# A two-layer hybrid trunk: where the GLA heads' projections stand in the order of work

## The chip, the cores and the metric

The kernel runs on one core of one Trainium2 chip. The time is the device time of one execution in microseconds; less is better. TensorE (PE) multiplies matrices, VectorE (DVE) and ScalarE (ACT) do the rest, GpSimd (POOL) a little, and SyncE (SP) issues the loads.

## The reference, cut to what matters

Two layers over 512 tokens (256 context, 256 latent) of width 1024; the second layer needs the latent tokens' outputs alone. Each layer has three token mixers side by side and an MLP:

```python
lx, ly, gq, gk, gv, gr, gz, aq, ak, av, bg = split(h @ w_in)
y1 = rglru_branch(lx, ly, ...)    # convolution, gates, two linear scans (one a direction)
y2 = gla_branch(gq, gk, gv, gr, gz, ...)   # 4 heads, two directions, chunks of 64
y3 = gqa_branch(aq, ak, av, ...)
x = x + ga1 * merge_branches(y1, y2, y3, bg, w_branch, w_out)
x = x + ga2 * squared_relu_mlp(...)
# gla_branch, one head and direction:
g = log_sigmoid(z @ gate_w + gate_b) / 16; b = cumsum(g) in a chunk
scores = tril((q * exp(b - b_mid)) @ (k * exp(b_mid - b)).T)
o = scores @ v + (q * exp(b)) @ s_prev
s = exp(b_last) * s + (k * exp(b_last - b)).T @ v
y2 = rms_norm(o) * silu(r)
```

## The kernel before

Everything is float32. A projection is multiplied as three products of a high and a low part in the float32r type: `weight` (L191) loads one tile of 128 x 1024 into `wraw`, ACT rounds it to `wh` (L200), DVE subtracts to `wl` (L201); three buffers each. `gemm` (L252) makes 24 matmuls of one tile into one of four PSUM banks of the pool `ps_mm`. `gemm_tok` (L276) makes four token blocks at once, 96 matmuls of 512 columns over four weight tiles, and takes all four banks. Layer 1 asks for 256 columns where only latent tokens are needed.

Temporaries come from three pools: `tmp` (`t2`, ten tiles of 128x512), `tmp1` (`t1`, fifteen of 128x256) and `gtmp` (`g2`, three of 128x512, used for the gate tiles of `merge` and in the MLP). An instruction that takes a tile waits until a tile of its pool is free. Each engine, and SP's queue of loads, runs its own list in order. The lists are drawn up when the kernel is built: program order gives the priority (`weight` moves its load and split some 800 instructions ahead), and what is not ready by the builder's own estimate gives way to what is.

The RG-LRU loop (L621) goes over eight channel tiles in pairs: `lru_conv` is a GEMM with a four-tap convolution on ACT and DVE, `lru_gates` four float32 matmuls (eight matmul instructions) with Tanh on ACT, `lru_decay` Exp on ACT, then one Sqrt for the pair (L630), some `gate_y` GEMMs, and `lru_scan` on DVE with a cast on ACT (L293). After pair 2 comes `gla_z`: it loads and splits a small weight (`wz`, `wzs`) and multiplies z (L568). After pair 6 come `gla_gates(0)`: gate matmuls (L598), Abs, Exp and Ln on ACT (L601 to L605), scans on DVE.

Then `gla(h)` runs for four heads: its gates, the K GEMM with an ACT copy (L653), the Q GEMM with an ACT copy (L656), V by `gemm_tok` for each two heads with ACT copies (L661); for each direction the decayed products on DVE and ACT (L677 to L710), the scores (L715, L717), the transposes of the decayed K (L728) into `kt`, and the state products (L741); then the outputs (L760), their norm (L762 to L767, with a power on POOL at L136), and for each half the R GEMM with its SiLU (L771, L772), the transposes (L775), and the product into y2 (L776). After heads 1 and 2 four `merge` calls each multiply y1 by its branch weight (two GEMMs, a Tanh at L787, a product on DVE). Attention follows: keys and values first, then queries, with merges between. Where the trace calls a tile `mm` it is a GEMM's bank, `mx` a bank of the other four, `t` a temporary, `lru` the RG-LRU's work tiles, `yp` the halves of y in layer 1.

In layer 1 the modulation of the layer is still being summed on DVE between this work; its loads (L330) stand in SP's queue among the weights and take `t2` tiles.

Of the kernel before, what the change touches and what calls it, by code (L numbers as in the profile page):

```python
# [15 lines left out]
F32 = mybir.dt.float32  # L16
F32R = mybir.dt.float32r
# [12 lines left out]
QORD = "q0mmfq1mmmfummm", "q0mmfq1mmmmmmf"  # L30
WSPB, EBB, G2B, WRB = 3, 1, 3, 3
NSPL = 5
# [4 lines left out]
NHP = 800  # L37
GZP, G0P = 2, 6
AHEAD = 800
# [65 lines left out]
def trunk_kernel(ctx: ExitStack, tc: tile.TileContext, out: bass.AP, d: dict):  # L105
# [47 lines left out]
    G.memset(cs, 0.0)  # L153
    c8 = const.tile([128, KT, 2], F32, name="c8")
    nc.sync.dma_start(c8, d["cs"])
# [7 lines left out]

    pick = const.tile([128, 2, 32], F32, name="pick")
    G.memset(pick, 0.0)
    for b in range(2):
        G.memset(pick[:, b, b:b + 1], 1.0)

# [4 lines left out]

    th = const.tile([128, KT, 2], F32, name="th")
    S.activation(th, c8, AF.Tanh, scale=0.5)
# [145 lines left out]
    def mods(l, us, pace, nd=KT):  # L321
# [19 lines left out]
        for u, j in halves:  # L341
            bs = (0, 1) if l == 0 or u < 2 else (1,)
            acc = [tmp() for _ in bs]
            terms = [(pick[:, b, :], a) for a, b in zip(acc, bs)]
            nx = load(u, j, 0)
            for k in range(KT):
                t, nx = nx, load(u, j, k + 1) if k + 1 < KT else None
                if k >= nd:
                    terms.append((cs[:, k, :], t))
                    continue  # L350
                for a, b in zip(acc, bs):
                    c = cs[:, k, b:b + 1]
                    if k == 0:
                        S.activation(a, t, AF.Copy, scale=c)
                    else:
                        V.scalar_tensor_tensor(a, t, c, a, op0=ALU.mult, op1=ALU.add)  # L356
# [91 lines left out]
    c2 = const.tile([128, NL, 2, 16], F32, name="c2")  # L448
    lam = const.tile([128, NL, 16], F32, name="lam")
    la = const.tile([128, NL, 16], F32, name="la")  # L450
    lb = const.tile([128, NL, 16], F32, name="lb")
    lc = const.tile([128, NL, 16], F32, name="lc")
    lo_, hi_ = PCOLS["lam"]
    V.tensor_copy(lam, par[:, :, lo_:hi_])
    S.activation(la, lam, AF.Abs)
# [15 lines left out]

    habx = const.tile([128, NL, 32], F32, name="habx")
    lo_, _ = PCOLS["ab"]
    _, hi_ = PCOLS["xb"]
    V.tensor_scalar(habx, par[:, :, lo_:hi_], 0.5, None, op0=ALU.mult)

    for l in range(NL):
# [62 lines left out]
        def lru_scan(i):  # L540
# [15 lines left out]
            split_to(y1h[:, i, c0:], y1l[:, i, c0:], y)  # L556

        def gla_z():


            wz = tmp1(F32, (128, KT, 32))
            nc.sync.dma_start(wz, d["wz"][l])
            wzs = t2.tile([128, KT, 64], F32R, name="wzs", tag="t2")
            split_to(wzs[:, :, :32], wzs[:, :, 32:], wz)
            pz = mx()
# [21 lines left out]
        def gla_gates(h):  # L587
# [26 lines left out]
            return bs  # L614

        LYS = LYS0, LYS1
        ly = iter(range(8))
# [3 lines left out]
        for i in range(0, 8, 2):  # L621
            lru_conv(i + 1)
            lru_gates(i)
            if i < 6:
                lru_conv(i + 2)
            lru_gates(i + 1)
            for j in range(2):
                lru_decay(i + j)
            tt = ws_[1][:, i % 4:i % 4 + 2]
            S.activation(tt, tt, AF.Sqrt, scale=0.25, bias=epsc)  # L630
            for j in range(LYS[l][i // 2 + 1]):
                gate_y(next(ly))
            for j in range(2):
                lru_scan(i + j)
            if i == GZP:
                zs = gla_z()
            if i == G0P:
                gates0 = gla_gates(0)

# [5 lines left out]

        v2 = {}

        def gla(h):
            bs = gla_gates(h) if h else gates0

            pk = gemm(weight(l, "in", O_GK + 128 * h), hh, hl, 0)
            k_ = tmp()
            cp(E_K)(k_, pk)  # L653
            pq = gemm(weight(l, "in", O_GQ + 128 * h), hh, hl, c0)
            q_ = tmp()
            S.activation(q_[:, c0:], pq, AF.Copy, scale=128.0 ** -0.5)  # L656
            if h % 2 == 0:
                for t, ps in gemm_tok(l, O_GV + 256 * h, hh, hl, range(4)).items():
                    for a in range(2):
                        v2[h + a, t] = tmp1()  # L660
                        cp(E_V)(v2[h + a, t], ps[:, 256 * a:256 * a + 256])  # L661
            v_ = [v2.pop((h, t)) for t in range(4)]

            lo = c0 // 64
            nq = 8 - lo
            t0 = c0 // 128
            st = [[None] * 4 for _ in range(2)]
            pts, qhs = [], []
            for dd in range(2):
# [57 lines left out]
                for t in seq[:3]:  # L727
                    P.transpose(pkt[:, 128 * t:128 * t + 128], kh[:, 128 * t:128 * t + 128], ident)  # L728
                kt = tmp()
                if dd == 0:  # L730
                    cp(E_KT)(kt[:, :384], pkt[:, :384])
                else:
                    S.copy(kt[:, :256], pkt[:, :256])
                    S.copy(kt[:, 384:], pkt[:, 384:])
                cur = None
                for j, t in enumerate(seq):
# [28 lines left out]
            for t in range(t0, 4):  # L765
                o = on[t - t0]
                V.tensor_scalar(o, o, rs[:, t:t + 1], None, op0=ALU.mult)  # L767
            for j in range(2):
                pr = gemm(weight(l, "in", O_GR + 256 * h + 128 * j), hh, hl, c0)
                y = tmp()  # L770
                S.activation(y[:, c0:], pr, AF.Tanh, scale=0.5)  # L771
                V.scalar_tensor_tensor(y[:, c0:], y[:, c0:], 1.0, pr, op0=ALU.add, op1=ALU.mult)  # L772
                po = mx()
                for t in range(t0, 4):
                    P.transpose(po[:, 128 * t:128 * t + 128], on[t - t0][:, 128 * j:128 * j + 128], ident)  # L775
                V.scalar_tensor_tensor(y[:, c0:], po[:, c0:], hg[:, j:j + 1], y[:, c0:],  # L776
                                       op0=ALU.mult, op1=ALU.mult)
                split_to(y2h[:, 2 * h + j, c0:], y2l[:, 2 * h + j, c0:], y[:, c0:])

# [15 lines left out]

        m = x[:, :, :256] if last else bigp.tile([128, KT, T], F32, name="big")
        for h in range(4):
            gla(h)
            for i in range(MG[l][h], MG[l][h + 1]):
                merge(0, i, y1h, y1l)  # L800
# [28 lines left out]
        for t, ps in gemm_tok(l, O_AK, hh, hl, range(4)).items():  # L829
# [5 lines left out]
            V.tensor_copy(a, ps[:, 256:])  # L835
            av.append(a)
        rsk = sm.tile([128, 8], F32, name="rsk")
        rsqrt(rsk, ssk, 1.0 / 128, EPS)
# [299 lines left out]
```

## Time and profile before

| what | value |
|---|---|
| median of 3 runs | 1898.92 us (1896.93 to 1903.13) |
| profiled execution | 1897.52 us; its span 1895.7 us |
| busy: PE | 1810.9 us (96%) |
| busy: DVE | 1282.9 us (68%) |
| busy: ACT | 924.8 us (49%) |
| mean granted TensorE clock | 0.989 of full |

The span reaches from the first to the last instruction. Matmuls are pipelined and their ends are modelled, so that PE's share is above its rate of work; a hole is told by the idle time in front of an instruction, which stands in brackets behind its row with what ended it.

### The profile page before, as it was taken

The page shows a single profiled execution, that of the slowest core. Times are in us where ns is not written, and L with a number is a line of the kernel's source. Part 1 is how long each engine was busy: PE and PEld are TensorE (multiplying, and loading weights), DVE is VectorE, ACT ScalarE, POOL GpSimd, SP SyncE. Part 2 cuts the span into 40 slices and gives each one's busy share as a digit, 9 for nine tenths or more (in the row PEclk, how much of TensorE's full clock was granted, in tenths as well). Part 3 has the DMA queues.
Part 4 walks back from the last instruction along what each step waited for, and adds up shares of the span by engine and source line. Part 5 has one row for each costly group of instructions (what it writes and reads, how often), then busy time and mean ns, then how long its engine had stood idle before and what let it go on. Part 6 is the DMA issues. An engine that isn't in the chain of part 4 may idle for free.

```text
span 1895.7 us, 26828 instructions
## 1 busy us (share of the span) xinstructions
PE 1810.9 (96%) x10248; PEld 1509.6 (80%) x10248; DVE 1282.9 (68%) x2177; ACT 924.8 (49%) x1586; POOL 57.1 (3%) x88
## 2 busy tenths in 40 slices
PE   5998999999999999999999999996999999999999
PEld 4765778887777888988888889764888878998887
DVE  5677764535566767789744448787765668577877
ACT  3778544334434333564232325876654554455443
POOL 1000000000000000000000001000000000000000
PEclk9999999999999999999999999998999999999999
DMA  9322223222211566666633335531343333664664
GB/s 318 99 74 73 69 69 90 77 93 78 72 51 56 190 193 196 222 224 199 211 109 97 98 102 185 164 114 61 130 122 111 122 123 91 234 193 150 190 190 154
DMA packets 91617, 255.62 MB, mean 135 GB/s; under 512 B 9184, under 2 KB 20576, under 8 KB 91488
## 3 DMA queue, kind: packets, MB, share of 16 engines
q1 hardware_dynamic: 91488, 253.90, 42.6%
q8 instruction: 81, 1.33, 0.3%
q14 instruction: 48, 0.39, 0.1%
HBM read 252.82 MB, written 1.05 MB: 134 GB/s over the span
## 4 chain that ended last, share of the span: by engine, by line
issue 49%; PE 39%; DVE 5%; ACT 4%; POOL 2%; DMA 0%; SPq 0%; POOLq 0%; ACTq 0%; DVEq 0%
PE mm L212 31%; PE mx L212 2%; PE mx L760 1%; PE mx L741 1%; DVE wl L201 1%; ACT wh L200 1%; PE mx L715 1%; PE mx L526 1%; POOL t L425 1%; PE mx L216 1%; DVE lru L546 0%; PE mx L717 0%; DVE lru L545 0%; ACT lru L630 0%; ACT lru L527 0%
## 5 line engine op out<-in xcount | busy, mean ns | idle before, releaser
L212 PE MATMUL mm<-h,wh 128*128 128x512 f32 (+1 forms) x2640 | 733.3, 360 | 8.3 <-DVE wh L198 4.5
L200 ACT CAST wh<-wraw 128x1024 fp32r<-128x1024 f32 x363 | 379.8, 1049 | 544.3 <-PE mm L212 465.3
L201 DVE TENSOR_TENSOR wl<-wraw,wh 128x1024 fp32r<-128x1024 f32 x365 | 445.8, 1223 | 257.6 <-ACT wh L200 254.2
L212 PEld LDWEIGHTS mm<-h,wh 128*128 128x128 f32 x2640 | 468.3, 189 | 85.4 <-issue 6.6
L212 PE MATMUL mm<-h,wl 128*128 128x512 f32 (+1 forms) x1448 | 493.2, 341 | 0.0
L212 PEld LDWEIGHTS mm<-h,wl 128*128 128x128 f32 x1448 | 273.8, 189 | 31.9 <-issue 1.4
L212 PE MATMUL mm<-yh,wh 128*128 128x512 f32 (+1 forms) x640 | 224.7, 351 | 2.4 <-DVE big L957 2.4
L212 PE MATMUL mm<-yh,wl 128*128 128x512 f32 (+1 forms) x640 | 224.3, 350 | 0.0
L212 PE MATMUL mm<-yl,wh 128*128 128x512 f32 (+1 forms) x640 | 222.6, 348 | 0.0
L212 PE MATMUL mm<-wh,h 128*128 128x512 f32 x576 | 187.3, 400 | 18.5 <-ACT t L653 18.1
L212 PE MATMUL mm<-yp,wh 128*128 128x256 f32 (+1 forms) x704 | 186.0, 338 | 3.8 <-ACT g L787 2.3
L212 PE MATMUL mm<-yp,wl 128*128 128x256 f32 x512 | 144.4, 282 | 0.0
L356 DVE SCALAR_TENSOR_TENSOR t<-t,cs,t 128x512 f32<-128x512 f32 x178 | 127.2, 746 | 24.1 <-DMA t<-mod_w 15.1
L212 PEld LDWEIGHTS mm<-wh,h 128*128 128x128 f32 x576 | 109.7, 191 | 42.3 <-ACT t L653 18.9
L212 PEld LDWEIGHTS mm<-yp,wh 128*128 128x128 f32 x704 | 120.8, 191 | 20.1 <-ACT g L787 2.5
L212 PEld LDWEIGHTS mm<-yh,wh 128*128 128x128 f32 x640 | 121.6, 190 | 17.8 <-issue 3.4
L212 PEld LDWEIGHTS mm<-yh,wl 128*128 128x128 f32 x640 | 121.2, 189 | 15.3 <-issue 0.7
L212 PEld LDWEIGHTS mm<-yl,wh 128*128 128x128 f32 x640 | 121.2, 189 | 15.0 <-issue 0.5
L212 PE MATMUL mm<-wl,h 128*128 128x512 f32 x288 | 115.2, 400 | 2.0 <-DVE wl L201 2.0
L212 PEld LDWEIGHTS mm<-yp,wl 128*128 128x128 f32 x512 | 97.1, 190 | 1.0 <-issue 1.0
L212 PE MATMUL mx<-t,t 128*128 128x128 f32 (+2 forms) x416 | 81.8, 338 | 0.0
L957 DVE SCALAR_TENSOR_TENSOR big<-mm,modT,big 128x256 f32<-128x256 f32 x64 | 28.6, 480 | 66.8 <-PE mm L212 66.8
(226 smaller groups left out, 1987.4 us busy)
## 6 DMA issues: line engine op xcount, KB each, us to landing
wraw<-wt SPq DMA_DIRECT2D x365, 512.0 KB, 3.6
t<-mod_w SPq DMA_DIRECT2D x144, 256.0 KB, 3.8
modw<-mod_w SPq DMA_DIRECT2D x6, 2048.0 KB, 14.1
big<-xt SPq DMA_DIRECT2D x8, 512.0 KB, 5.3
gw<-lruw SPq DMA_DIRECT2D x16, 256.0 KB, 3.5
out<-big SPq DMA_DIRECT2D x8, 128.0 KB, 2.5
t<-glaw SPq DMA_DIRECT2D x8, 96.0 KB, 3.1
t<-ropeg SPq DMA_DIRECT2D x2, 256.0 KB, 3.0
```

The source lines that it names most:

```text
L200: S.copy(wh, r)
L201: (G if lo == "G" else V).tensor_tensor(wl, r, wh.bitcast(F32), op=ALU.subtract)
L212: P.matmul(o, a, b, **kw)
L216: P.transpose(o, a, ident)
L356: V.scalar_tensor_tensor(a, t, c, a, op0=ALU.mult, op1=ALU.add)
L425: G.tensor_tensor(h[:, :n], x[:, k, c0:c1], st[1][:, :n], op=ALU.mult)
L526: P.matmul(pg, gw[:, 2 * dd + q, :], xc, start=True, stop=True)
L715: P.matmul(psc[:, c], en[:, c], em[:, c], start=True, stop=True)
L741: P.matmul(pu[:, :256], kt[:, 128 * t:128 * t + 128], v_[t], start=True, stop=True)
L760: P.matmul(po[:, :256], a, b, start=j == 0, stop=j == len(mm) - 1)
L957: V.scalar_tensor_tensor(x[:, i, c], ps[:, 256 * s - a:256 * s - a + 256], s0[:, i, s:s + 1], x[:, i, c], op0=ALU.mult, op1=ALU.add)
```

## The change

In both layers: the small weight of z is loaded and split at the layer's start, into a tile of the pool `g2`. In the last pair of the RG-LRU loop the order becomes: channel 7's convolution, K and Q of head 0, gates of channel 6, head 0's gates, V of heads 0 and 1, gates of channel 7, decays, Sqrt, the two R GEMMs of head 0 with their SiLU, the scans. `gla(h)` makes R ahead of the scores; its state products come behind both directions' scores; and its end (transposes of the output, the product into y2) is returned as a function, which the next head calls behind its K and Q, or, after head 3, attention behind its key and value copies. `kt` and R's product come from `g2`, which gets a fourth tile. To make room, some constants of the start are temporaries, `pick` is smaller and `habx` is computed in place.

```diff
-WSPB, EBB, G2B, WRB = 3, 1, 3, 3
+WSPB, EBB, G2B, WRB = 3, 1, 4, 3
...
+        wz = tmp1(F32, (128, KT, 32))
+        nc.sync.dma_start(wz, d["wz"][l])
+        wzs = g2.tile([128, KT, 64], F32R, name="wzs", tag="g2")
+        split_to(wzs[:, :, :32], wzs[:, :, 32:], wz)
+
         def gla_z():
...
-            wz = tmp1(F32, (128, KT, 32))
-            nc.sync.dma_start(wz, d["wz"][l])
-            wzs = t2.tile([128, KT, 64], F32R, name="wzs", tag="t2")
-            split_to(wzs[:, :, :32], wzs[:, :, 32:], wz)
...
+        def gla_kq(h):
+            pk = gemm(weight(l, "in", O_GK + 128 * h), hh, hl, 0)
+            k_ = tmp()
+            cp(E_K)(k_, pk)
+            pq = gemm(weight(l, "in", O_GQ + 128 * h), hh, hl, c0)
+            q_ = tmp()
+            S.activation(q_[:, c0:], pq, AF.Copy, scale=128.0 ** -0.5)
+            return k_, q_
...
+        def gla_r(h):
+            ys = []
+            for j in range(2):
+                pr = gemm(weight(l, "in", O_GR + 256 * h + 128 * j), hh, hl, c0)
+                y = gtmp()
+                S.activation(y[:, c0:], pr, AF.Tanh, scale=0.5)
+                V.scalar_tensor_tensor(y[:, c0:], y[:, c0:], 1.0, pr, op0=ALU.add, op1=ALU.mult)
+                ys.append(y)
+            return ys
...
             lru_conv(i + 1)
-            lru_gates(i)
             if i < 6:
+                lru_gates(i)
                 lru_conv(i + 2)
+            else:
+                kq0 = gla_kq(0)
+                lru_gates(i)
+                gates0 = gla_gates(0)
+                v0 = gla_v(0)
             lru_gates(i + 1)
...
+            if i == 6:
+                ys0 = gla_r(0)
             for j in range(2):
                 lru_scan(i + j)
             if i == GZP:
                 zs = gla_z()
-            if i == G0P:
-                gates0 = gla_gates(0)
...
+            if h:
+                bs = gla_gates(h)
+                k_, q_ = gla_kq(h)
+                before()
+                v_ = gla_v(h)
+                ys = gla_r(h)
+            else:
+                bs, (k_, q_), v_, ys = gates0, kq0, v0, ys0
...
-                kt = tmp()
+                kt = gtmp()
...
+                kts.append((kt, decp))
+            for dd, (kt, decp) in enumerate(kts):
+                seq = (0, 1, 2, 3) if dd == 0 else (1, 0, 3, 2)
                 cur = None
...
-            for j in range(2):
-                pr = gemm(weight(l, "in", O_GR + 256 * h + 128 * j), hh, hl, c0)
...
+            def end():
+                for j, y in enumerate(ys):
+                    po = mx()
...
+        end = None
         for h in range(4):
-            gla(h)
+            end = gla(h, end)
...
             av.append(a)
+        end()
```

## Rows read from the trace of the kernel before

**Rows 1.** Windows of both layers: span, busy PE, PEld, DVE, ACT, POOL, clock, DMA
```profile
140.00:475.00 335.00, 317.92 (x1462) 256.97 (x1461) 195.29 (x300) 169.63 (x288) 11.15 (x21) 0.99 0.25 78
1262.00:1530.00 268.00, 241.69 (x1375) 203.07 (x1374) 182.32 (x322) 158.72 (x279) 9.43 (x21) 0.96 0.36 112
```
**Rows 2.** Chain that ended last: start, duration, what; both layers, GEMMs without holes
```profile
369.04 43.57 PE mm L212 x192
...
1459.21 17.99 PE mm L212 x150
```
**Rows 3.** Order of time, PE, layer 0: start, duration, instruction, count, [idle before, releaser]
```profile
157.04 1.03 PE L212 MATMUL mm<-h,wh 128*128 128x512 f32 x2
...
169.21 3.67 PE L526 MATMUL mx<-t,gw 128*128 128x512 f32 x8 [1.61 <-issue]
...
190.09 0.79 PE L212 MATMUL mm<-wh,h 128*128 128x512 f32 x1 [7.65 <-ACT t L653]
```
**Rows 4.** Window of GEMM matmuls (L212) alone: span, PE busy (count), PEld busy, clock
```profile
174.12:182.45 8.33, 8.32 (x37) 6.57 (x35) 1.00 0.27 90
```
**Rows 5.** Order of time, ACT, layer 0, end of the RG-LRU
```profile
177.20 1.28 ACT L630 ACT_TABLE_LOAD   x1
178.50 2.01 ACT L630 ACTIVATE lru<-lru,epsc 128x2048 f32<-128x2048 f32 x1
...
185.33 1.06 ACT L605 ACTIVATE eb<-eb 128x1024 f32<-128x1024 f32 x1
188.93 0.62 ACT L293 CAST yh<-lru 128x512 fp32r<-128x512 f32 x1 [2.54 <-DVE lru L555]
189.46 0.58 ACT L653 COPY t<-mm 128x512 f32<-128x512 f32 x1
```
**Rows 6.** Order of time, PE, layer 1, end of the RG-LRU
```profile
1296.96 6.33 PE L526 MATMUL mx<-t,gw 128*128 128x512 f32 x8 [4.11 <-DVE t L515]
...
1318.27 0.79 PE L212 MATMUL mm<-wh,h 128*128 128x512 f32 x1 [10.41 <-ACT t L653]
```
**Rows 7.** Windows behind the long holes; columns as rows 1
```profile
190.09:193.11 3.02, 3.02 (x7) 2.40 (x8) 3.02 (x6) 0.44 (x1) 0.00 (x0) 0.53 0.03 5
...
1318.27:1322.97 4.70, 4.70 (x12) 3.69 (x12) 4.70 (x8) 0.24 (x1) 0.00 (x0) 0.52 0.02 3
```
**Rows 8.** Waits, layer 0 then 1: us in total, times, longest; ends of heads
```profile
PE mx L775 <- DVE t L767: 3.8, 4, 1.0
...
PE mx L775 <- DVE t L767: 2.3, 4, 0.7
```
**Rows 9.** Waits, layer 0; then order of time, PE, layer 1: scores and merges
```profile
PE mx L715 <- DVE t L709: 2.5, 2, 1.3
...
1367.81 0.50 PE L212 MATMUL mm<-yp,wh 128*128 128x256 f32 x2 [1.50 <-ACT t L653]
1376.13 0.50 PE L212 MATMUL mm<-yp,wh 128*128 128x256 f32 x2 [2.30 <-ACT g L787]
1378.82 1.20 PE L715 MATMUL mx<-t,t 128*128 128x128 f32 x4 [1.18 <-DVE t L709]
```
**Rows 10.** Order of time, PE, both layers: first matmul of z
```profile
128.23 0.66 PE L568 MATMUL mx<-h,wzs 128*64 128x512 f32 x1 [2.62 <-DVE wzs L294]
...
1257.09 0.42 PE L568 MATMUL mx<-h,wzs 128*64 128x512 f32 x1 [1.37 <-DVE wzs L294]
```
**Rows 11.** Order of time, DVE: operands of head 0's first scores, and a wait
```profile
204.42 0.68 DVE L709 TENSOR_TENSOR t<-t,t 128x512 f32<-128x512 f32 x1
...
1309.47 1.29 DVE L545 SCALAR_TENSOR_TENSOR lru<-lru 128x512 f32<-128x512 f32 x2 [4.73 <-ACT lru L630]
...
1334.74 0.41 DVE L710 TENSOR_TENSOR t<-t,t 128x256 f32<-128x256 f32 x1
```
**Rows 12.** Window of GEMM matmuls (L212), head 0, layer 0, scores to output; as rows 4
```profile
206.96:226.28 19.32, 10.19 (x38) 6.90 (x38) 1.00 0.30 88
```
**Rows 13.** Waits of SP's queue in layer 1: us in total, times, longest
```profile
SPq L330 <- DVE lru L555: 18.6, 1, 18.6
```

More of the change, by code (lines that the diff above doesn't have):

```diff
@@ L37 @@
 NHP = 800
-GZP, G0P = 2, 6
+GZP = 2
 AHEAD = 800
@@ L153, in trunk_kernel @@
     G.memset(cs, 0.0)
-    c8 = const.tile([128, KT, 2], F32, name="c8")
+    c8, th = (tmp1(shape=(128, KT, 2)) for _ in range(2))
     nc.sync.dma_start(c8, d["cs"])
@@ L161, in trunk_kernel @@
     G.memset(epsc, 1e-30)
-    pick = const.tile([128, 2, 32], F32, name="pick")
+    pick = const.tile([128, 33], F32, name="pick")
     G.memset(pick, 0.0)
-    for b in range(2):
-        G.memset(pick[:, b, b:b + 1], 1.0)
+    G.memset(pick[:, 1:2], 1.0)
     def pc(l, name, a=0, n=None):
@@ L171, in pc @@
         return par[:, l, lo + a:hi if n is None else lo + a + n]
-    th = const.tile([128, KT, 2], F32, name="th")
     S.activation(th, c8, AF.Tanh, scale=0.5)
@@ L343, in mods @@
             acc = [tmp() for _ in bs]
-            terms = [(pick[:, b, :], a) for a, b in zip(acc, bs)]
+            terms = [(pick[:, 1 - b:33 - b], a) for a, b in zip(acc, bs)]
             nx = load(u, j, 0)
@@ L448, in trunk_kernel @@
     c2 = const.tile([128, NL, 2, 16], F32, name="c2")
[L449 to L452, printed above, removed]
+    la, lb, lc = (tmp1(shape=(128, NL, 16)) for _ in range(3))
     lo_, hi_ = PCOLS["lam"]
-    V.tensor_copy(lam, par[:, :, lo_:hi_])
+    lam = par[:, :, lo_:hi_]
     S.activation(la, lam, AF.Abs)
@@ L469, in trunk_kernel @@
     V.tensor_scalar(c2[:, :, 1, :], lam, 2.0, None, op0=ALU.mult)
-    habx = const.tile([128, NL, 32], F32, name="habx")
     lo_, _ = PCOLS["ab"]
     _, hi_ = PCOLS["xb"]
-    V.tensor_scalar(habx, par[:, :, lo_:hi_], 0.5, None, op0=ALU.mult)
+    habx = par[:, :, lo_:hi_]
+    V.tensor_scalar(habx, habx, 0.5, None, op0=ALU.mult)
     for l in range(NL):
@@ L614, in gla_gates, with gla_v @@
             return bs
+        v2 = {}
+        def gla_kq(h):
[6 more added lines that the diff above has]
+            return k_, q_
+        def gla_v(h):
+            if h % 2 == 0:
+                for t, ps in gemm_tok(l, O_GV + 256 * h, hh, hl, range(4)).items():
+                    for a in range(2):
+                        v2[h + a, t] = tmp1()
+                        cp(E_V)(v2[h + a, t], ps[:, 256 * a:256 * a + 256])
+            return [v2.pop((h, t)) for t in range(4)]
+        def gla_r(h):
[7 more added lines that the diff above has]
+            return ys
         LYS = LYS0, LYS1
@@ L644, in trunk_kernel, with gla @@
         y2h, y2l = ytiles("yl")
[L646 to L662, printed above, removed]
+        def gla(h, before=None):
+            if h:
[6 more added lines that the diff above has]
+                bs, (k_, q_), v_, ys = gates0, kq0, v0, ys0
             lo = c0 // 64
@@ L667, in gla @@
             st = [[None] * 4 for _ in range(2)]
-            pts, qhs = [], []
+            pts, qhs, kts = [], [], []
             for dd in range(2):
@@ L767, in gla @@
                 V.tensor_scalar(o, o, rs[:, t:t + 1], None, op0=ALU.mult)
-            for j in range(2):
-                pr = gemm(weight(l, "in", O_GR + 256 * h + 128 * j), hh, hl, c0)
[L770 to L778, printed above, removed]
+            def end():
+                for j, y in enumerate(ys):
+                    po = mx()
+                    for t in range(t0, 4):
+                        P.transpose(po[:, 128 * t:128 * t + 128], on[t - t0][:, 128 * j:128 * j + 128], ident)
+                    V.scalar_tensor_tensor(y[:, c0:], po[:, c0:], hg[:, j:j + 1], y[:, c0:],
+                                           op0=ALU.mult, op1=ALU.mult)
+                    split_to(y2h[:, 2 * h + j, c0:], y2l[:, 2 * h + j, c0:], y[:, c0:])
+            return end
         m = None
```

## The prediction, made before the changed kernel ran

> **What bounds the kernel now.** I read first the engines' busy time in the two stretches that the change touches, one a layer, from the last RG-LRU gates to the end of the GLA heads [rows 1]. PE is busy for 317.9 of 335 us and 241.7 of 268; DVE for 195.3 and 182.3, ACT for 169.6 and 158.7. TensorE sets the pace, and what an order of work can win is its holes, 17.1 and 26.3 us, and what it lost at half clock behind them. How fast it goes without holes stands in the chain of waits [rows 2]: 192 matmuls in 43.57 us are 0.227 us each (512 columns), 150 in 17.99 are 0.120 (256 columns). A GEMM of one weight tile has 24: 5.4 us over 512 tokens, 2.9 over the 256 of layer 1.
>
> Then PE's order of time, for holes. In layer 0 [rows 3]: 1.61 us ahead of channel 7's gates and 7.65 in the middle of head 0's V, waiting for ACT's copy of K (L653). PE had made K and Q from 157.04, ahead of gates (169.21) that stand before them in the program: the order is put together from what is ready, not taken from the text. V has 96 matmuls over four PSUM banks; 36 were done (the window's 37 hold one of Q) [rows 4] when it needed the banks of K and Q. ACT's order of time tells why they were still held [rows 5]: the square root until 180.5, head 0's Exp and Ln until 186.4, then 2.54 idle behind a cast that waits for the scan on DVE, and only then, at 189.46, the copy of K that could have run 25 us before. Layer 1 has the same holes, larger [rows 6]: 4.11 and 10.41, and the eight gate matmuls after the first took 6.33 us where layer 0 took 3.67. The windows show the granted clock there at about half of full [rows 7], that is 1.2 for 2.4 GHz. The other holes are regular: ahead of the transposes at each head's end, 3.8 and 2.3 us over four heads each [rows 8]; ahead of some heads' scores and layer 1's merges [rows 9]; ahead of the rank-16 gates' z, behind the split of wzs [rows 10].
>
> **The change part by part**, in us of the profiled execution.
>
> (a) wzs is loaded and split at the layer's start instead of in front of z. Both waits go: 2.62 + 1.37 = 4.0. Its load and two small operations move ahead of the first GEMMs, past SP's first weights; that costs between 0 (beside them) and 2.6 (the same wait elsewhere). I take 0.3, since the split is now wanted tens of us later. Gain 3.7.
>
> (b) Layer 0, K and Q with their copies ahead of gates 6, head 0's gates and V ahead of gates 7, R ahead of the scans. The stop goes: 1.61 + 7.65, and the restart at half clock: 7 matmuls took 3.02 [rows 7] against 1.59, so 1.43. Together 10.7. What is late next are head 0's scores. From 182.4 the other 60 V matmuls take 13.6, to 196.0; the two R GEMMs, now next, 48 x 0.227 = 10.9, to 206.9. DVE ended the first direction's operands at 205.1 [rows 11]. So the scores hardly wait, but DVE gets R's two products ahead of the scans, queued behind PE: I keep 10.
>
> (c) Layer 1, the same edits: 4.11 + 10.41, gates at half clock 6.33 - 3.67 = 2.66, restart 4.70 of which some 4.4 at half clock [rows 7], so 2.2. Together 19.4. Here the scores do wait. V stood at 36 of 96 at 1307.9; without 4.11 and 2.66 that is 1301.1, V's end 1314.7, R's (48 x 0.120) 1320.5. DVE had the operands at 1335.2 [rows 11], 14.7 later. The next head's K and Q can fill 5.4 + 2.9 = 8.3, leaving 6.4; DVE's own idle 4.73 behind the square root can go, which leaves 1.7; a stop of that kind costs up to 2.2 more at half clock. Between 0 and 8.6; I take 4. Gain 15.4.
>
> (d) A head's end goes behind the next head's keys, the last one's behind attention's keys and values. The 3.8 + 2.3 = 6.1 are now covered by a GEMM of 5.4 or more. Its products are wanted only by the second branch's merges. It holds two SBUF tiles a head longer (see g). If the order leaves too little between, the 6.1 come back. I take 5.6.
>
> (e) R ahead of the scores gives each head 10.9 or 5.8 us more work before its scores: the 2.5 of layer 0 and two times 1.18 of layer 1 go [rows 9], 4.9. Layer 1's merges waited 1.50 for a late K copy and 2.30 for a gate tile; no edit is aimed at them, 0 to 3.8, and I take 0.6. Gain 5.5.
>
> (f) The price of (b) and (e): R was what PE did between a head's scores and its output, where it else waits for DVE and ACT. In head 0 of layer 0 there were 38 such matmuls in that stretch [rows 12], 8.6 us; at 0.120 in layer 1 4.6. If nothing takes their place: 4 x 8.6 + 4 x 4.6 = 52.8; if all is replaced: 0. The next head's K and Q (10.9, 8.3) stand right behind, merges behind heads 1 and 2, attention's K and V behind head 3, and [rows 3] show that GEMMs are drawn ahead. So nearer to 0: I take 10.
>
> (g) Kt and R's products move to the pool of the merges' gate tiles, four instead of three. While a head is in its state products it holds two Kt and two R: a merge can be multiplied into PSUM, but not be evacuated. Two merges fill the four banks, 21.8 and 11.5 us of work, against a stretch of 19.3 [rows 12]: no wait in layer 0, up to 7.8 at heads 1 and 2 of layer 1. 0 to 15.6; I take 3, since Kt is free before the output.
>
> The constants that become temporaries, the state products behind both directions' scores and the smaller pick tile move no GEMM: 0, beside PE's work.
>
> ACT changes function sets more: head 0's Exp and Ln now stand between the gates' Tanh of channels 6 and 7. One load takes 1.28 us and the next operation follows 0.02 later [rows 5]. At most two more a layer, 5.1 us of an engine that is 51% and 59% busy [rows 1]: 0 on the path. The Trainium skill, ScalarE: Activation LUTs, section Table sets: the hidden batching unit, tells one to group functions by set, which this change goes against, and puts a switch at about 2.66 us with its drain. By that price ACT would have 10.6 us more; the row shows no drain.
>
> **Sum.** 3.7 + 10 + 15.4 + 5.6 + 5.5 - 10 - 3 = 27.2. The profiled execution took 1897.5, and the median is 1.4 above that; 1898.9 - 27.2 = 1871.7, and I forecast 1871.
>
> **The rivals.**
>
> Nothing takes R's place (slower): between scores and output PE idles for DVE and ACT in every head, all 52.8 of (f). The time is 1871 + 42.8 = 1914. It is slower than before from 37 us of the 52.8 on, some 70%. For it: PSUM has four banks for GEMMs, and R's last two are freed only by DVE, which is full there. Against it: [rows 3], and that ACT alone frees K and Q. Chance 0.09.
>
> The stalls move: scores of layer 1 late by the whole 8.6 (4.6 more than charged) and merges held by (g) (12.6 more): 1888. For it: R's products, which wait for PE, now stand ahead of the scans on DVE, and everything of head 0 that DVE does comes after. Chance 0.17.
>
> It doesn't do what it says: K and Q are still copied late, because the pool of ten 512-column tiles is full. For it: a modulation load, which needs such a tile, held SP's queue for 18.6 us in layer 1 [rows 13]. Then 7.65 + 1.43 + 10.41 + 2.2 = 21.7 stay, less the 4.7 already charged on them: 1888. Against it: Kt, R and wzs leave that pool. Chance 0.11.
>
> ACT's loads fall on the path: 5.1 more, 1876. By the page's price named above it would be 10.6 more. Chance 0.05.
>
> All is covered: (f), (g) and the charges in (c) and (e) are nothing, 20 less: 1851. Chance 0.13.
>
> **How the numbers follow.** The forecast has the other 0.45, and its own range is 1860 to 1880. A measurement tells 0.3% from no change, 5.7 us, so faster is below 1893.2. The forecast, full cover and ACT's loads lie there (0.63); of the moved stalls 0.14, of the late copies 0.07: 0.84. Same: 0.03 + 0.04, and 0.01 of the slower one: 0.08. Slower: 0.08. The range 1850 to 1894 leaves out the slower rival (0.09), half of the full cover's spread and a little of the late copies: about 0.16.
>
> **What would show it.** Right: the copy of K follows its GEMM within a few us; no hole over 2 us between channel 7's convolution and head 0's scores in either layer; the granted clock stays at full from gates 7 on; the transposes at a head's end no longer wait for the scaling by the norm; z has no wait. Wrong: PE waiting for head 0's operands by more than 4 us, PE waiting between scores and output (f), merges' matmuls waiting for their gate tiles (g), or the K copy still behind the scan's cast. The prediction fails if PE's order is drawn up so that it has nothing else ready in the heads.

## The result, and the profile after

The changed kernel took 1873.01 us (median of 4 runs, 1869.75 to 1874.93), the kernel before 1900.49 in the runs beside it (4, 1896.93 to 1903.13): a ratio of 0.9855, 95% interval 0.9832 to 0.9878. It is 27.5 us faster; the forecast was 1871. The profiled execution took 1873.47 us with a span of 1871.7.

First the page's engines after the change, then the windows that answer to [rows 1], shifted so that they hold nearly the same work (1448 matmuls for 1462 and 1376 for 1375; span, busy PE, PEld, DVE, ACT, POOL, clock, DMA):

```profile
PE 1806.8 (97%) x10248; PEld 1513.2 (81%) x10248; DVE 1277.6 (68%) x2176; ACT 926.3 (49%) x1586; POOL 65.6 (4%) x87
```

```profile
140.00:455.00 315.00, 309.64 (x1448) 254.32 (x1446) 189.78 (x295) 162.99 (x279) 17.77 (x21) 1.00 0.27 84
1241.40:1500.00 258.60, 236.93 (x1376) 204.51 (x1374) 179.07 (x314) 154.92 (x269) 10.81 (x21) 0.95 0.36 112
```

Layer 0's window has 5.4 us of holes where [rows 1] had 17.1. Layer 1's still has 21.7, where it had 26.3, and its clock fell from 0.96 to 0.95: layer 0 was put right, layer 1 hardly.

How far the layers differ is read from two landmarks on PE that are the same work in every kernel: the first gate matmul of channel 0, and the first transpose of attention's keys. The stretch between them, one a layer:

| kernel | layer 0 | layer 1 |
|---|---|---|
| before | 65.1 to 476.2: 411.1 | 1200.4 to 1529.0: 328.6 |
| after | 64.1 to 455.4: 391.3 | 1179.5 to 1501.4: 321.9 |
| gain | 19.8 | 6.7 |

Behind the second landmark there are 366.7 us before and 370.3 after. No edit reaches there, and in the fourteen kernels shown here that part lies between 366.1 and 371.0. The same program for layer 0 gave its stretch 391.3 here, 391.5, 392.8 and 394.1 in others (pair_mix, v_late1 and scan_late1 below). Each stretch comes from one profiled execution, so a difference under some 3 us tells nothing by itself.

PE's order of time in layer 0 after the change, its only holes above 0.5 us from 150 us to the end of the heads; and ACT's copy of K (start, duration, instruction, count, [idle before, releaser]):

```profile
165.75 1.08 PE L595 MATMUL mx<-zs,t 96*128 96x512 f32 x2 [2.77 <-ACT lru L522]
...
223.67 1.16 PE L743 MATMUL mx<-t,t 128*128 128x128 f32 x8 [0.72 <-DVE t L737]
...
254.72 1.16 PE L743 MATMUL mx<-t,t 128*128 128x128 f32 x8 [0.83 <-DVE t L738]
```

```profile
157.52 0.58 ACT L619 COPY t<-mm 128x512 f32<-128x512 f32 x1
```

The copy of K is made at 157.52, not at 189.46 [rows 5], and the hole of 7.65 in V [rows 3] is gone. In its place stands 2.77 ahead of head 0's gates, released by ACT's Tanh of channel 6 (L522). There is no wait above 0.5 us at the heads' ends, at z, or between a head's second scores and its output; the 0.72 and 0.83 stand ahead of scores.

Layer 1 (L743 are the scores, made for a head's first and then its second direction; L521 here channel 7's gates, L210 a merge):

```profile
1290.55 3.59 PE L521 MATMUL mx<-t,gw 128*128 128x512 f32 x8
...
1299.73 0.61 PE L743 MATMUL mx<-t,t 128*128 128x128 f32 x4
...
1324.97 1.22 PE L743 MATMUL mx<-t,t 128*128 128x128 f32 x4 [9.62 <-DVE t L737]
...
1343.53 0.80 PE L210 MATMUL mm<-yp,wh 128*128 128x256 f32 x2 [3.29 <-ACT t L619]
...
1356.01 1.23 PE L743 MATMUL mx<-t,t 128*128 128x128 f32 x4 [4.05 <-DVE t L738]
...
1362.29 1.19 PE L743 MATMUL mx<-t,t 128*128 128x128 f32 x4 [3.60 <-DVE t L737]
```

The holes of 4.11 and 10.41 [rows 6] have gone. Head 0's first scores run at 1299.73 without a wait, but 9.62 stands ahead of its second, and head 1's scores wait 4.05 and 3.60, where 1.18 stood [rows 9]. Windows of that stretch (columns as above), and DVE's order of time in it:

```profile
1285.00:1303.00 18.00, 18.00 (x106) 14.27 (x105) 9.20 (x17) 15.48 (x26) 0.42 (x2) 1.00 0.39 117
1303.00:1325.00 22.00, 12.38 (x91) 11.37 (x90) 21.61 (x39) 9.97 (x16) 0.92 (x2) 0.85 0.39 121
...
1345.00:1365.00 20.00, 12.35 (x66) 11.09 (x66) 15.38 (x33) 7.76 (x14) 1.38 (x4) 0.67 0.27 83
```

```profile
1287.24 0.43 DVE L737 TENSOR_TENSOR t<-t,t 128x256 f32<-128x256 f32 x1
...
1302.75 1.29 DVE L540 SCALAR_TENSOR_TENSOR lru<-lru 128x512 f32<-128x512 f32 x2 [3.51 <-ACT lru L665]
...
1324.49 0.42 DVE L737 TENSOR_TENSOR t<-t,t 128x256 f32<-128x256 f32 x1
```

In the first window PE has no hole and DVE idles for 8.8 of 18 us; in the second DVE is full and PE idles for 9.6 of 22. So the work came to DVE late. DVE's rows show from where: it had the operands of head 0's first scores at 1287.7 (L737); then the scans of channels 6 and 7 (L540) wait for the square root (L665), and the last operand of the second scores (L737 again, 1324.49) comes behind them.

### The profile page after: what moved, and what is told of

The parts are those of the page before. It is cut to its first block, busy times and chain, and to the rows that moved or that the text cites. A ratio compares the mean times of both kernels' runs of the same rounds, so it can differ in the third digit from the quotient of the medians.

```text
span 1871.7 us, 26774 instructions
## 1 busy us (share of the span) xinstructions
PE 1806.8 (97%) x10248; PEld 1513.2 (81%) x10248; DVE 1277.6 (68%) x2176; ACT 926.3 (49%) x1586; POOL 65.6 (4%) x87
## 5 line engine op out<-in xcount | busy, mean ns | idle before, releaser
L210 PE MATMUL mm<-h,wh 128*128 128x512 f32 (+1 forms) x2640 | 730.4, 360 | 6.4 <-DVE wh L196 3.4
L210 PEld LDWEIGHTS mm<-h,wh 128*128 128x128 f32 x2640 | 468.3, 189 | 85.5 <-issue 6.4
L210 PE MATMUL mm<-h,wl 128*128 128x512 f32 (+1 forms) x1448 | 493.9, 341 | 0.1
L210 PEld LDWEIGHTS mm<-h,wl 128*128 128x128 f32 x1448 | 274.2, 189 | 32.3 <-DVE wl L199 1.2
L210 PE MATMUL mm<-yh,wh 128*128 128x512 f32 (+1 forms) x640 | 224.8, 351 | 2.9 <-ACT wh L198 2.9
L210 PE MATMUL mm<-yh,wl 128*128 128x512 f32 (+1 forms) x640 | 224.1, 350 | 0.0
L210 PE MATMUL mm<-yl,wh 128*128 128x512 f32 (+1 forms) x640 | 222.6, 348 | 0.0
L210 PE MATMUL mm<-yp,wh 128*128 128x256 f32 (+1 forms) x704 | 189.2, 342 | 3.3 <-ACT t L619 3.3
L210 PE MATMUL mm<-wh,h 128*128 128x512 f32 x576 | 183.5, 395 | 0.0
L210 PE MATMUL mm<-yp,wl 128*128 128x256 f32 x512 | 145.9, 285 | 0.0
L210 PEld LDWEIGHTS mm<-yp,wh 128*128 128x128 f32 x704 | 122.1, 193 | 20.3 <-ACT t L619 3.5
L210 PEld LDWEIGHTS mm<-yh,wh 128*128 128x128 f32 x640 | 121.6, 190 | 18.3 <-ACT wh L198 3.1
L210 PEld LDWEIGHTS mm<-yh,wl 128*128 128x128 f32 x640 | 121.2, 189 | 15.5 <-issue 0.7
L210 PEld LDWEIGHTS mm<-yl,wh 128*128 128x128 f32 x640 | 121.2, 189 | 14.9 <-issue 0.5
L210 PEld LDWEIGHTS mm<-wh,h 128*128 128x128 f32 x576 | 107.8, 188 | 22.3 <-issue 0.7
L210 PE MATMUL mm<-wl,h 128*128 128x512 f32 x288 | 113.1, 393 | 0.0
L210 PEld LDWEIGHTS mm<-yp,wl 128*128 128x128 f32 x512 | 98.2, 192 | 1.0 <-issue 1.0
L210 PE MATMUL mx<-t,t 128*128 128x128 f32 (+2 forms) x416 | 81.7, 338 | 0.1
```

The lines of the kernel that those rows point to most:

```text
L210: P.matmul(o, a, b, **kw)
```

## The experiments

Every run below is set beside the kernel before on the same chip. Each part of the change was undone alone (wz_back, end_back, r_back, pair_back), the pair's order was put into the kernel before without the moves of R, ends and load (pair_alone) and into layer 0 alone (pair_mix), and the wait of 9.62 was attacked in four ways (scan_late1, t2_11, kq_first, v_late1 and v_late2); gates_ahead goes at what was left in head 1. The stretches are those of the table above. By the intervals end_back, r_back and pair_alone are slower than the changed kernel. Those of v_late1 and v_late2 touch its own at the edge, and each of their runs (at most 1868.58) was faster than each of its runs (1869.75 and up). The other intervals overlap with its own, so that what is said of these kernels rests on the stretches and on the waits in the rows.

| kernel | median, us | ratio to before, 95% | layer 0 | layer 1 |
|---|---|---|---|---|
| after | 1873.01 | 0.9855 (0.9832 to 0.9878) | 391.3 | 321.9 |
| wz_back | 1871.85 | 0.9858 (0.9838 to 0.9878) | 391.5 | 322.0 |
| end_back | 1882.42 | 0.9911 (0.9889 to 0.9934) | 397.3 | 324.2 |
| r_back | 1888.49 | 0.9940 (0.9918 to 0.9962) | 400.4 | 326.1 |
| pair_back | 1877.16 | 0.9885 (0.9862 to 0.9908) | 401.9 | 317.8 |
| pair_alone | 1892.43 | 0.9948 (0.9929 to 0.9967) | 405.3 | 326.7 |
| pair_mix | 1868.07 | 0.9831 (0.9816 to 0.9846) | 391.5 | 317.8 |
| scan_late1 | 1870.66 | 0.9842 (0.9814 to 0.9871) | 394.1 | 320.0 |
| t2_11 | 1873.57 | 0.9856 (0.9831 to 0.9880) | 392.3 | 320.8 |
| kq_first | 1873.08 | 0.9850 (0.9828 to 0.9872) | 392.5 | 320.4 |
| v_late1 | 1867.12 | 0.9821 (0.9806 to 0.9836) | 392.8 | 313.5 |
| v_late2 | 1865.29 | 0.9814 (0.9795 to 0.9833) | 394.0 | 312.2 |
| gates_ahead | 1867.37 | 0.9832 (0.9815 to 0.9848) | 394.1 | 312.0 |

### wz_back: the small weight loaded in front of z again

```diff
-        wz = tmp1(F32, (128, KT, 32))
-        nc.sync.dma_start(wz, d["wz"][l])
-        wzs = g2.tile([128, KT, 64], F32R, name="wzs", tag="g2")
-        split_to(wzs[:, :, :32], wzs[:, :, 32:], wz)
         def gla_z():
+            wz = tmp1(F32, (128, KT, 32))
+            nc.sync.dma_start(wz, d["wz"][l])
+            wzs = g2.tile([128, KT, 64], F32R, name="wzs", tag="g2")
+            split_to(wzs[:, :, :32], wzs[:, :, 32:], wz)
```

> The changed kernel with the load and the split of z's small weight back in front of z (its tile stays in the larger pool). Forecast's term (a): 3.7 us slower than the changed kernel, so about 1877, with waits of some 2.6 us (layer 0) and 1.4 us (layer 1) ahead of z's first matmul. Rival: the wait was hidden anyway by what else DVE does there and returns as a wait elsewhere: within 1 us of 1873.

Neither stretch moved, and z has no wait in either layer. pair_alone too has its z without a wait with the load in front of it and the tile in `g2`. So the wait of 4.0 [rows 10] is gone, but not through the move; what both runs keep is, among other things, the tile's other pool, with its fourth tile, and `kt` out of `t2`. No run put either back into `t2`, so that this is the cause is not shown.

### end_back: a head's end directly behind its norm

```diff
-                before()
...
-            return end
+            end()
...
-            end = gla(h, end)
+            gla(h)
...
-        end()
```

> The changed kernel with each head's end straight behind its outputs, as before. Forecast's term (d): 5.6 us slower than the changed kernel, about 1879, with eight waits of 0.3 to 1 us for the scaling by the norm. Rival: with R already done, nothing stands between the outputs and the end's transposes, so that each wait is longer than before, 2 us and more a head: about 1890.

9.4 us slower than the changed kernel by the medians, 6.0 + 2.3 by the stretches. PE's waits, layer 0's heads and then layer 1's (us in total, times, longest; L803 are the ends' transposes, L742 the scores):

```profile
PE mx L803 <- DVE t L797: 2.8, 3, 1.0
PE mx L742 <- DVE t L736: 2.6, 3, 1.0
PE mx L803 <- ACT g L817: 1.0, 1, 1.0
```

```profile
PE mx L803 <- DVE t L797: 2.7, 4, 0.8
```

The ends' waits are back with 3.8 in layer 0 and 2.7 in layer 1; [rows 8] had 3.8 and 2.3. The scores of layer 0 wait 2.6 instead of 1.6. That is 7.5 of the 8.3.

### r_back: R behind the scores again

```diff
-            if i == 6:
-                ys0 = gla_r(0)
...
-                ys = gla_r(h)
...
-                bs, (k_, q_), v_, ys = gates0, kq0, v0, ys0
+                bs, (k_, q_), v_ = gates0, kq0, v0
...
+            ys = gla_r(h)
```

> The changed kernel with the two R GEMMs of every head behind its outputs again, head 0's too. By the forecast's (e) and (f) R's place costs 10 - 5.5, so this kernel is up to 4.5 us faster than the changed one, about 1869, with waits ahead of the scores back in layer 0. Rival from the trace of after: in layer 0 R ahead of the scores costs nothing (no hole between scores and output), and R's 10.9 and 5.8 us are wanted ahead of the scores: slower by 5 to 15 us, 1878 to 1888.

15.5 us slower than the changed kernel, 9.1 + 4.2 by the stretches. PE's order of time at head 0's second scores, layer 0 and layer 1:

```profile
221.53 2.08 PE L740 MATMUL mx<-t,t 128*128 128x128 f32 x8 [6.47 <-DVE t L734]
```

```profile
1332.84 1.20 PE L740 MATMUL mx<-t,t 128*128 128x128 f32 x4 [12.13 <-DVE t L734]
```

Without R ahead of a head's scores head 0's second ones wait 6.47 instead of 0.72, and 12.13 instead of 9.62. R is worth more ahead of the scores than behind them.

### pair_back: the old order of the last gates, all else kept

```diff
             lru_conv(i + 1)
+            lru_gates(i)
             if i < 6:
-                lru_gates(i)
                 lru_conv(i + 2)
-            else:
-                kq0 = gla_kq(0)
-                lru_gates(i)
-                gates0 = gla_gates(0)
-                v0 = gla_v(0)
             lru_gates(i + 1)
...
-            if i == 6:
-                ys0 = gla_r(0)
...
+            if i == 6:
+                gates0 = gla_gates(0)
...
+            bs = gla_gates(h) if h else gates0
+            k_, q_ = gla_kq(h)
             if h:
-                bs = gla_gates(h)
-                k_, q_ = gla_kq(h)
                 before()
-                v_ = gla_v(h)
-                ys = gla_r(h)
-            else:
-                bs, (k_, q_), v_, ys = gates0, kq0, v0, ys0
+            v_ = gla_v(h)
+            ys = gla_r(h)
```

> The changed kernel with the last RG-LRU pair in the order of before: head 0's gates behind the scans, its K, Q, V and R behind the loop; ends, R ahead of the scores and z's weight stay as changed. Forecast's (b) and (c): 25 us slower than the changed kernel, about 1898, nearly all of the gain lost, with PE waiting for the copy of K in both layers. Rival: the gain is spread, and this part holds less than half of it: below 1887.

Only 4.1 us slower, and the two layers go opposite ways: layer 0 loses 10.6, layer 1 gains 4.1. PE's order of time:

```profile
161.86 6.66 PE L521 MATMUL mx<-t,gw 128*128 128x512 f32 x8 [3.98 <-issue]
...
185.39 0.79 PE L210 MATMUL mm<-wh,h 128*128 128x512 f32 x1 [3.46 <-ACT t L619]
...
1301.98 0.79 PE L210 MATMUL mm<-wh,h 128*128 128x512 f32 x1 [10.30 <-ACT t L619]
...
1350.16 0.50 PE L210 MATMUL mm<-yp,wh 128*128 128x256 f32 x2 [1.50 <-ACT t L619]
...
1363.19 0.68 PE L735 MATMUL mx<-t,t 128*128 128x128 f32 x4 [1.25 <-DVE t L730]
...
1368.59 1.22 PE L735 MATMUL mx<-t,t 128*128 128x128 f32 x4 [3.87 <-DVE t L729]
```

The stops for the copy of K are back in both layers, 10.30 in layer 1 as in [rows 6]. And yet layer 1 is faster with that stop than with the new order: head 0's scores (here L735) don't wait at all, and the last three rows, head 1's late K copy and its two scores, are 1.50, 1.25 and 3.87, 6.6 in all, where the changed kernel has 3.29, 4.05 and 3.60, 10.9. So the new order exchanged a stop of 10.30 for a wait of 9.62 and made head 1 wait 4.3 longer.

### pair_alone: the pair's new order, but R, ends and load of z's weight where they were before

```diff
-WSPB, EBB, G2B, WRB = 3, 1, 3, 3
+WSPB, EBB, G2B, WRB = 3, 1, 4, 3
...
-            lru_gates(i)
             if i < 6:
+                lru_gates(i)
                 lru_conv(i + 2)
+            else:
+                kq0 = gla_kq(0)
+                lru_gates(i)
+                gates0 = gla_gates(0)
+                v0 = gla_v(0)
```

The diff is against the kernel before. The constants that make room, the pool of z's weight and of `kt`, and the state products behind both directions' scores are as in the changed kernel.

> The kernel before with the new order of the last RG-LRU pair alone (head 0's K, Q, gates and V among the gates): R behind the outputs, ends straight behind, z's weight in front of z. (State products stay behind both directions' scores, and the larger pool stays.) If the parts add up as the four runs before say (layer 0: 10 gained by the pair's order, layer 1: 4 lost), it is 6 us faster than before, about 1894. By the forecast's (b) and (c) it would be 25 us faster, 1875. Rival: without R ahead nothing covers head 0's scores in either layer and it is not faster than before at all: 1899 or more.

About 9 us faster than before: 5.8 in layer 0, 1.9 in layer 1, of which 2.6 and 1.4 may be z's waits. The holes ahead of head 0's second scores are those of r_back, 6.47 and 12.13. So the new order without R ahead of the scores is worth some 3 us in layer 0, with R 10.6.

### pair_mix: the new order in layer 0, the old one in layer 1

```diff
             if i < 6:
                 lru_gates(i)
                 lru_conv(i + 2)
+            elif last:
+                lru_gates(i)
             else:
...
-            if i == 6:
+            if i == 6 and not last:
                 ys0 = gla_r(0)
...
+            if i == 6 and last:
+                gates0 = gla_gates(0)
...
+                v_ = gla_v(h)
+                ys = gla_r(h)
+            elif last:
+                bs = gates0
+                k_, q_ = gla_kq(h)
```

> After's kernel with the new order of the last gates in layer 0 and the order of the kernel before in layer 1. With the old order in both layers TensorE reached the first key transpose of attention 10.2 us later in layer 0 but took 3.9 us less from there to that of layer 1. If the two layers add, this run is about 4 us faster than the changed kernel, 1869; the wait ahead of head 0's scores in layer 1 is then near 10 us as with the old order in both layers. If the gain in layer 1 came only from starting later, the time is the changed kernel's, 1873.

4.9 us faster than the changed kernel by the medians, and the stretches are just layer 0 of the one and layer 1 of the other, 391.5 and 317.8. The layers add. The stop for K stands in layer 1:

```profile
1290.73 0.80 PE L210 MATMUL mm<-wh,h 128*128 128x512 f32 x1 [10.30 <-ACT t L619]
```

### scan_late1: layer 1's last scans behind head 0's operands

```diff
+LATE = (False, True)
...
-                lru_scan(i + j)
+                if not (LATE[l] and i == 6):
+                    lru_scan(i + j)
...
+            if LATE[l] and h == 0:
+                for j in range(2):
+                    lru_scan(6 + j)
...
```

> The changed kernel, but in layer 1 the scans of channels 6 and 7 stand behind both directions' score operands of head 0 instead of ahead of them. Theory DVE: the hole of 9.6 us ahead of the second direction's scores is DVE working through 13 us of scans first; then the hole goes, and the time falls by 8 to 12 us to about 1862. Theory tiles: PE waits there because all four GEMM banks hold results (K, Q and R of head 1) that find no free temporary, so moving the scans only moves the hole: within 3 us of 1873.

In the changed kernel the scans do stand ahead of the second operands, but moving them behind is not enough. PE's order of time:

```profile
1322.62 0.71 PE L747 MATMUL mx<-t,t 128*128 128x128 f32 x4 [0.91 <-DVE t L742]
...
1330.23 1.22 PE L780 MATMUL mx<-t,g 128*128 128x256 f32 x2 [3.85 <-DVE t L785]
...
1333.72 4.41 PE L799 MATMUL mx<-t,t 128*128 128x256 f32 x12 [2.27 <-ACT yp L292]
```

The 9.62 is 0.91, and 3.85 and 2.27 appear in the state products and the output, which now have DVE's scans beside them. Layer 1's stretch is 1.9 shorter, within the scatter.

### t2_11: eleven tiles of 512 columns, thirteen of 256

```diff
-NT2, NT1 = 10, 15
+NT2, NT1 = 11, 13
```

> The changed kernel with eleven instead of ten 512-column temporaries (and thirteen instead of fifteen small ones, to make room). Theory tiles: head 1's K can be copied out earlier in layer 1, PE gets a bank and does part of head 1 or a merge in the hole: 3 to 10 us faster, 1863 to 1870. Theory DVE: nothing, or a little slower for the small tiles: 1871 to 1878.

The hole stays, so one tile more doesn't fill it; the wait for head 1's K copy stays too (3.30):

```profile
1324.76 1.22 PE L743 MATMUL mx<-t,t 128*128 128x128 f32 x4 [9.21 <-DVE t L737]
```

### kq_first: K and Q ahead of the gates in heads 1 to 3

```diff
             if h:
-                bs = gla_gates(h)
                 k_, q_ = gla_kq(h)
+                bs = gla_gates(h)
```

> The changed kernel with heads 1 to 3 making K and Q, with their copies, ahead of their gates. Theory order: head 1's K is copied late (29 us after its GEMM) only because its copy stands behind the head's Exp and Ln on ACT; then the waits for that copy go (3.3 us in layer 1) and some of the hole of 9.6 is filled: 4 to 10 us faster. Theory tiles: there is no tile for the copy, so nothing changes, and gates that come later make the holes ahead of head 1's scores longer: 0 to 5 us slower.

The wait of 3.29 for K's copy goes, and head 1's scores wait 7.42 instead of 4.05; 9.61 stays ahead of head 0's:

```profile
1327.12 1.22 PE L743 MATMUL mx<-t,t 128*128 128x128 f32 x4 [9.61 <-DVE t L737]
...
1355.66 1.22 PE L743 MATMUL mx<-t,t 128*128 128x128 f32 x4 [7.42 <-DVE t L738]
```

### v_late1 and v_late2: V behind channel 7's gates, in layer 1 and in both

```diff
                 gates0 = gla_gates(0)
+                if not (last):
+                    v0 = gla_v(0)
+            lru_gates(i + 1)
+            if i == 6 and (last):
                 v0 = gla_v(0)
-            lru_gates(i + 1)
```

v_late2 has the same with `True` for `last`.

> After's kernel with one edit: in layer 1 only, head 0's V stands behind gates 7 in the program instead of ahead of them. If V (about 21 us of TensorE with its copies) ahead of gates 7 is what puts back the square root, and with it the scans and the operands of head 0, then the scans start some 10 to 14 us earlier beside V, VectorE's idle time before them shrinks from about 9 us, the wait of 9.6 us ahead of head 0's scores in layer 1 falls under 3, and the kernel is 6 to 12 us faster than the changed one, 1861 to 1867. If it is the number of GEMM banks or the late copies of K and Q that leave TensorE with nothing, the wait of 9.6 stays or comes back elsewhere in the layer, and the time is within 3 us of the changed kernel's.

> After's kernel with head 0's V behind gates 7 in both layers. Layer 1 as in the run with the edit in layer 1 alone. In layer 0 the changed kernel has no wait above 2.8 us around the gates and 0.7 ahead of head 0's scores, so there is nothing to win: if V beside gates 7 covers something there (the stop for the copy of K that the kernel before had), a wait of 3 to 8 us comes back in layer 0 and the run is that much slower than the one with layer 1 alone; if not, the two are within 2 us.

v_late1 is 5.9 us faster than the changed kernel by the medians, and its layer 1 8.4 shorter. Of it, PE's order of time, the windows, and DVE's first scan:

```profile
1276.21 1.96 PE L521 MATMUL mx<-t,gw 128*128 128x512 f32 x4 [1.05 <-ACT eb L598]
...
1315.49 0.71 PE L746 MATMUL mx<-t,t 128*128 128x128 f32 x4 [1.26 <-DVE t L741]
```

```profile
1285.00:1303.00 18.00, 18.00 (x101) 15.10 (x100) 14.35 (x21) 16.80 (x26) 1.12 (x1) 1.00 0.35 103
1303.00:1325.00 22.00, 20.74 (x146) 18.91 (x145) 20.55 (x43) 10.82 (x21) 3.00 (x4) 1.00 0.45 144
```

```profile
1294.67 1.29 DVE L540 SCALAR_TENSOR_TENSOR lru<-lru 128x512 f32<-128x512 f32 x2 [1.77 <-ACT lru L668]
```

Channel 7's gates are on PE 14 us earlier, although this layer began 4.2 later; the scans start 8.1 earlier; DVE works 14.35 of the first 18 us instead of 9.20, and PE 20.74 of the next 22 instead of 12.38. Head 0's second scores don't wait, its first wait 1.26, and the clock is full in both windows. So V's place ahead of these gates is the cause of the 9.62. The move does two things, it starts the scans earlier and keeps V as PE's work beside them; no run parts the two. In layer 0 the same move (v_late2) brings no stop back and wins nothing: 394.0, where the changed kernel's own layer 0 gave 391.3 to 394.1. v_late2 has the lowest median of all, 1865.29, 35 us under the kernel before; it is not told apart from v_late1.

### gates_ahead: v_late2, and in layer 1 the next head's gates ahead of a head's state products

```diff
-                bs = gla_gates(h)
+                bs = gnext.pop(h, None) or gla_gates(h)
...
+            if last and h < 3:
+                gnext[h + 1] = gla_gates(h + 1)
             for dd, (kt, decp) in enumerate(kts):
```

> The kernel with head 0's V behind gates 7 in both layers, and in layer 1 the gates of heads 1 to 3 put ahead of the state products and the output of the head before instead of behind its output. Left in layer 1 are 3.3 us of TensorE for the late copies of head 1's K and Q, which ScalarE makes behind that head's Exp and Ln, and 4.0 and 3.6 for that head's operands, 10.9 in all. If they come from head 1's gates starting late, all three shrink, together to under 5, and the time is 4 to 8 us less, 1857 to 1861. If VectorE or the merges set it, or the gates' tiles held longer put off head 0's scores or its output, the waits only move and the time is within 3 us of 1865.3.

No gain: 1867.37, and layer 1's stretch is 312.0 for 312.2. PE's order of time in layer 1, first v_late2, then gates_ahead:

```profile
1320.48 2.75 PE L775 MATMUL mx<-t,g 128*128 128x256 f32 x12
...
1335.76 0.51 PE L210 MATMUL mm<-yp,wh 128*128 128x256 f32 x2 [3.30 <-ACT t L619]
...
1347.28 1.23 PE L746 MATMUL mx<-t,t 128*128 128x128 f32 x4 [4.01 <-DVE t L741]
...
1353.56 1.20 PE L746 MATMUL mx<-t,t 128*128 128x128 f32 x4 [3.60 <-DVE t L740]
```

```profile
1323.54 0.70 PE L595 MATMUL mx<-zs,t 96*128 96x512 f32 x2 [1.78 <-DVE t L592]
...
1324.50 4.21 PE L778 MATMUL mx<-t,g 128*128 128x256 f32 x10
...
1345.33 0.68 PE L747 MATMUL mx<-t,t 128*128 128x128 f32 x4 [0.90 <-DVE t L742]
...
1350.79 1.19 PE L747 MATMUL mx<-t,t 128*128 128x128 f32 x4 [3.92 <-DVE t L741]
```

3.30, 4.01 and 3.60 become 1.78, 0.90 and 3.92, and ten state products of head 0 take 4.21 where twelve took 2.75. These waits are 4.3 us less, and the stretch is no shorter. What would fill head 1 in layer 1 stays open.

## Why the prediction was right in its total and wrong in its parts

The forecast was 1871, measured were 1873.0. By its terms, with (a), (d), (e) and (f) shared between the layers as their rows are, it gave layer 0 some 12 us (2.4 + 10 + 3.5 + 2.5 - 6.5) and layer 1 some 15. The stretches gave 19.8 and 6.7. Two errors, some 8 us each and of opposite signs, cancelled: that the total came out is luck.

| term | forecast | undoing it alone cost, layer 0 and layer 1 |
|---|---|---|
| (a) wz early | 3.7 | 0, 0 |
| (b) pair's order, layer 0 | 10 | 10.6 |
| (c) pair's order, layer 1 | 15.4 | -4.1 |
| (d) ends | 5.6 | 6.0, 2.3 |
| (e) and (f) R ahead of the scores | 5.5 - 10 | 9.1, 4.2 |

**(c) is the step that failed.** It took over the time at which DVE had the operands of head 0's first scores, 1335.2 [rows 11], and asked only when PE would reach them; DVE's idle time behind the square root even counted as a gain. In the changed kernel these operands come ahead of the scans, at 1287.7, and the first scores don't wait. What waits are the second scores, whose operands DVE makes behind the scans. The new order put V, 22.5 us of PE in layer 1 (1268.07 to 1290.55), ahead of channel 7's gates, and Tanh, square root, scans and these operands follow one another behind the gates. Layer 1 begins 20.9 earlier than before, so the first scan, 1309.47 in [rows 11], should have come at 1288.6; it came at 1302.75, 14.2 later. The prediction costed V by its place on PE and not by what was queued behind it for the other engines. v_late1 shows it: with V behind these gates and all else kept, the 9.62 is gone and 1.26 is left, ahead of the first scores. Against the old order the term came out as a loss, by pair_back's rows: the stop of 10.30 became the wait of 9.62, and head 1 waits 4.3 longer. Layer 0 has a delay of the same kind (its square root ends at 198.7, in [rows 5] at 180.5) and no such hole. From there to the last operand of the second scores DVE takes about as long in both layers, 24.9 and 22.2 us; but PE has GEMM matmuls of 18.6 us between head 0's first and second scores in layer 0 and of 14.8 in layer 1, with R's 10.9 and 5.8 ahead of the first. That the columns make the difference between the layers is read from these numbers; no run tests it.

**(f) charged R's place for waits that are not there or have another cause.** Its stretch runs from a head's first scores to its output [rows 12]. In layer 0, where it put 6.5 of its 10, PE waits 0.72 there after the change; the next work does replace R, as the row of GEMMs drawn ahead [rows 3] had suggested. In layer 1 it waits 9.62 in head 0 and 3.60 in head 1, both ahead of second scores, and these are not R's price: r_back, with R behind the outputs, has 12.13 and 3.70 in the same places. The 3.60 is open. In the kernel before head 1's second scores don't wait; in all the others here they do, 2.34 to 3.92. What these share and no run undid is the place of the state products, which the prediction put at 0, the pool of `kt` and the constants. Nor was R's move a thing apart. (b) already counted on R between V and the scores, and pair_back and pair_alone show the pair's order worth 10.6 in layer 0 with R there and some 3 without. Terms that cover each other can't be added: (e) stood for 5.5, and undoing the move costs 13.3. Nor do the undone parts add up by layer: in layer 0 they cost 25.7 for a gain of 19.8, in layer 1 2.4 for a gain of 6.7, so that some 4 us of layer 1's gain are not traced to a part.

**(g)** charged 3 for merges held by the pool of four; no merge waits above 0.5 us for a gate tile after the change, and the 2.30 for one [rows 9] is gone.

**(d)** was right in kind and small in size: 5.6 for 8.3.

**(a)** forecast that z's waits go, which came, for a reason that doesn't hold: the move of the load is worth nothing by wz_back.

**ACT's loads.** The forecast allowed for two more loads of function sets a layer. The Trainium skill (ScalarE: Activation LUTs, Table sets: the hidden batching unit) asks that functions be grouped by set. The profile after has 43 loads of 1.28 us each, as many as before: the reordering added none, and so there was no price to pay.

**The rivals.** The rival of the moved stalls named the right place, layer 1's scores waiting for DVE, and gave 8.6 us for it, against 9.62 measured; its other half, merges held by (g), did not come, and layer 0 gained more than forecast, so its 1888 didn't either. The rival that nothing takes R's place is refuted: behind a head's second scores PE waits nowhere above 0.5 us up to its output, and with R put back there (r_back) the kernel is 15.5 slower. "Late copies" is refuted for head 0 by 157.52. Head 1 of layer 1 has a late copy, 3.29, but not for want of a tile: the wait goes in kq_first and stays in t2_11.

Of the prediction's signs, the early copy of K, the ends without waits and z without a wait came; "no hole over 2 us" failed in both layers, with 2.77 in layer 0 and 9.62, ahead of head 0's second scores, in layer 1, where the clock from gates 7 on did not stay at full either (0.85 from 1303 to 1325). Of its signs of being wrong, PE waiting for head 0's operands by more than 4 us came, in layer 1; and since it stands between first and second scores, it is a wait between scores and output too.

## What to carry to other kernels

When independent work is pulled forward on the busiest engine, look at what it is pulled in front of: a short operation that feeds a long chain on another engine (here eight gate matmuls of 3.6 us) should leave first, and the long block go behind it. That won 8.4 us in layer 1, where PE's other work did not cover the delay, and nothing in layer 0, where it did. Undo each part alone and by stage: a total that fits can be the sum of a part that works and one that hurts. And don't add up gains that use the same work as cover.

## What the runs showed that was not expected

The same new order of the last pair gains 10.6 us in layer 0 and loses 4.1 in layer 1, with the same operations; the likely reason, not tested, is that half as many columns shorten PE's cover (18.6 to 14.8 us) while DVE's chain stays about as long (24.9 and 22.2). And a hole on PE can cost more than its length: in the changed kernel the window from 1345 to 1365 us, with the scores' waits of 4.05 and 3.60 in it, shows a granted clock of 0.67, and v_late1's window from 1303 to 1325 shows 1.00 where the changed kernel's, with the hole of 9.62, shows 0.85. The four matmuls behind that hole take 1.22 us; head 0's first four, in a window at full clock, take 0.61.
